# Weight sums staged by whole groups, and four more groups by seven, in a hybrid attention block

## The chip, the cores and the metric

One core of one Trainium2 chip runs the kernel. The metric is the device time in microseconds (us) of the whole kernel, lower is better. Engines are named TensorE (PE in the profile), VectorE (DVE), ScalarE (ACT), GpSimd (POOL) and SyncE (SP, which issues nearly all DMAs).

## The reference

Everything is float32; `S` = 256 tokens, `D` = 2048. Cut to what matters:

```python
h = rms_norm(x, g_mix)
proj = h @ w_in                                   # 2048 x 11014: three attentions' inputs and the gates
o_fox, o_sb, o_mem = forgetting(...), stick_breaking(...), memory(...)   # 6, 6 and 4 heads of 128
g = sigmoid(gates.reshape(b, s, 3, D) + b_gate)
merged = g[0] * (o_fox @ w_br_fox) + g[1] * (o_sb @ w_br_sb) + g[2] * (o_mem @ w_br_mem)
x = x + merged @ w_out                            # 2048 x 2048
u = causal_depthwise_conv(rms_norm(x, g_ffn) @ w_up, conv_w, conv_b)     # 2048 x 11264, 3 taps
u_gate, u_val = split(u, 2)
x = x + (silu(u_gate) * u_val) @ w_down           # 5632 x 2048
```

## The kernel before, in words

**Products.** Each float32 matrix is split in two parts, `hi` (rounded by a cast on ScalarE) and `lo` (the rest, subtracted on VectorE). A product of two matrices is three matmuls, high by high, low by high and high by low (`three`, lines 284 to 288). Weights arrive in pieces of 1024 columns per partition (512 KB): a DMA on SyncE into one of four `raw` slots, a cast into one of four `hi` slots, a subtraction into one of four `lo` slots, then TensorE. The four slots are how far the supply may run ahead.

**Stages, in order.** Memory keys and values with the transposes of `x`; the projections `mq`, `f0` to `f4`, `s0` to `s4` (16 k-tiles each, by twos); the gates and the branch products; the output stage (`w_out`, 16 groups); the up stage (`w_up` with convolution); the down stage (`w_down`, 44 groups). In the last stages a group is a pair of k-tiles against 1024 output columns and both token tiles.

**Groups by eight and by seven.** The plans (`o_plans`, `g_plans`, `d_plans`, lines 225 to 227) give a letter for each step. `e`: a group by the ordinary eight block products (`eight`, line 346). `s`: a group by seven, in Winograd's form of Strassen's scheme (`seven`, line 369): it multiplies sums of weight blocks with sums of activation blocks and collects four of its products in four more banks `Y`, which `gather` (line 305) folds into the residual after the last `s` of a half. A group by seven needs three and a half pieces of weights where one by eight needs two. `f` (`form`, line 1213): VectorE and ScalarE form the activation sums of one group (`pair_sums`, line 290), in `sf` or in place of activations that are no longer needed.

**Weight sums ahead of time.** The sums of weight blocks that `seven` reads are made beforehand and kept in DRAM (`sums_of`, tiles `kept_o`, `kept_d`). `weight_sums` (line 243) is a generator that works on half a group (256 columns of each block) at a time: two loads into a 4 KB per partition tile `pre`, three additions on VectorE, one store.

**Who does it when.** `tick` is called after each piece pair of a product, that is after every second k-tile of a projection or of the up stage. It advances every generator in `background` by one `yield`, and at most two of the queue `later` (heads, transposes, `x_sums`). So `period`, `store`, `add` and `delay` count ticks. `in_order` fixes an instruction's place among those so marked; the others are placed by the scheduler. In gate blocks no background generator is advanced. Before, one generator runs from `mq` to the end of the branches with period 6 (8 from the first gate block on), and two, with a tile each (`end0`, `end1`, which later hold the last activations), run in the up stage with period 8, store at tick 6, and delays of 22 and 24 ticks.

**Slots.** Tiles with one tag share a slot, and the later waits for the earlier one's last use. `xres` first holds `x`, then the activation sums `xs` of the gates, then `x` again. `x_sums` (line 842) forms `xs` after the forgetting heads.

Of the kernel before, what the change touches and what calls it, by code (L numbers as in the profile page):

```python
# [9 lines left out]
F32 = mybir.dt.float32  # L10
# [5 lines left out]
P = 128  # L16
# [19 lines left out]
BLOCKS = 14  # L36
WINDOW = 2
GS = 3


@with_exitstack
def hybrid_block(
# [54 lines left out]
    def later(gen):  # L97
        waiting.append(gen)
# [24 lines left out]
    def finish():  # L123
        while waiting or active:
            tick(beside=False)
# [96 lines left out]

    o_plans = ("eessesse", "eesesese")
    g_plans = (("", "", "esesesee"), ("esesesee", "esesesee", "esesesee"))
    d_plans = ("ef" * 5 + "ssef" * 4 + "seeee", "efefefesssfe" + "ssse" * 2 + "ssssee")
    T1, T3, T4, T2 = range(4)
    FS2, FS4, FS3, FS1 = range(4)
    in_order = tc.keep_in_program_order  # L230
# [9 lines left out]
        for h in range(2)  # L240
    )

    def weight_sums(staging, period, store, end=None, delay=0, slower=0, add=0):


        for _ in range(delay):
            yield
        while halves and end not in issued:
            name, wv, nb, pr, h = halves.popleft()
            at = f"{name}{nb}_{pr}"  # L250
            if h == 0:
                sums_of[name, nb, pr] = dram.tile([P, 4, 512], F32, tag=f"kept_{at}", name=f"kept_{at}")
            kept = sums_of[name, nb, pr]
            w = staging(f"pre_{at}_{h}").rearrange("p (i c) -> p i c", i=4)
            n0 = nb * PIECE + h * 256
            for n in range(2):
                in_order(
                    nc.sync.dma_start(
                        w.rearrange("p (k n) c -> p k n c", k=2)[:, :, n],
                        wv[:, 2 * pr : 2 * pr + 2, n0 + n * 512 : n0 + n * 512 + 256],  # L260
                    )
                )

            for _ in range(add):
                yield
            both = w[:, 1:2].to_broadcast([P, 2, 256])
            in_order(nc.vector.tensor_tensor(w[:, 0:2], w[:, 0:4:3], both, ALU.add))
            in_order(nc.vector.tensor_tensor(w[:, T2], w[:, T1], w[:, T2], ALU.add))
            in_order(nc.vector.tensor_tensor(w[:, T4], w[:, T2], w[:, T4], ALU.add))
# [20 lines left out]
    def pair_sums(pair, w, groups):  # L290

        v = pair.bitcast(F32).rearrange("p k (l c) -> p k l c", l=2)
        a, r = (half.rearrange("p (i q) -> p i q", i=4) for half in (w[:, :512], w[:, 512:]))
        nc.vector.tensor_tensor(w[:, :512].rearrange("p (k c) -> p k c", k=2), v[:, :, 0], v[:, :, 1], ALU.add)

        a10 = a[:, 1:2].to_broadcast([P, 2, P])
        nc.vector.tensor_tensor(r[:, FS3 : FS1 + 1], a[:, 0:4:3], a10, ALU.subtract)
        nc.vector.scalar_tensor_tensor(r[:, FS2], r[:, FS1], -1.0, a[:, 0], ALU.mult, ALU.subtract)
        nc.vector.tensor_tensor(r[:, FS4], r[:, FS2], a[:, 2], ALU.add)
        for dst, which in groups:  # L300
            nc.scalar.copy(dst[..., 0, :], r[:, which])
        for dst, which in groups:
            nc.vector.tensor_tensor(dst[..., 1, :], r[:, which], dst[..., 0, :].bitcast(F32), ALU.subtract)
# [143 lines left out]
    mv = mem[0].rearrange("(t p) d -> p t d", p=P)  # L447
    memres = xt_pool.tile([P, NT, D], F32, tag="xt", name="memres")

    def load_rows(q, srcs, name):  # L450

        n = sum(r for _, r in srcs)
        rows = cst.tile([n, P], F32, name=f"rows_{name}")
# [43 lines left out]
    taps = cst.tile([P, 4, 2 * FT], F32, name="taps")  # L497

    def constants():
        rows = cst.tile([2 * KT + 4, P], F32, name="rows_mix")  # L500
# [220 lines left out]
    def weighted(pT, v, h, oh, o):  # L721
# [6 lines left out]


    ps = proj(C_MQ, MEM_W, "mq")  # L730
    background.append(
        weight_sums(lambda name: gp.tile([P, 1024], F32, tag="pre", bufs=1, name=name), 6, 4, "merged", slower=2, add=2)
    )
    finish()
    qm = heads_of(block("qm"))
    y = norm_heads(ps, rstd, "mq")
    later(heads_T(y, qm, (gh[:, 2:3], gh[:, 2:3]), 2, "mq"))
# [99 lines left out]
        yield  # L837
        weighted(pT, vf, h, h, A)

    xs = cst.tile([P, GS, 4, 2, P], F32R, tag="xres", name="xs")  # L840

    def x_sums():
        for p in range(GS):
            pair_sums(xT.pair(p), block(f"xw_{p}"), [(xs[:, p], slice(0, 4))])
            yield 2

    later(running_sums())
    for h in range(N_FOX):
        later(fox_head(h))
    later(x_sums())  # L850


    qs = [None] * 3
    vs = [None] * 2
# [51 lines left out]
        later(sb_head(h))  # L906

    ps = proj(C_SB + 1536, 512, "s3")
    vs[0] = rows_of(block("vs0"))
    for t in range(NT):  # L910
        nc.scalar.activation(vs[0][:, t], ps[t], AF.Copy, scale=rstd[:, t : t + 1])
# [117 lines left out]


    hT = k_tiles("hT")
    rbc = cst.tile([P, S], F32, name="rbc")

    def hidden_T(n):
        yield
# [42 lines left out]

    FA = FT - 4
    aT = ff.tile([P, FA, 2 * S], F32R, bufs=1, name="aT")  # L1080
    ends = {}
    for i in range(2):
        background.append(
            weight_sums(
                lambda name, i=i: ff.tile([P, 1024], F32, tag=f"end{i}", bufs=1, name=name), 8, 6, delay=22 + 2 * i
            )
        )

    def a_pair(p):
        if p < FA // 2:  # L1090
            return aT[:, 2 * p : 2 * p + 2]
        if p not in ends:
            ends[p] = ff.tile([P, 2, 2 * S], F32R, tag=f"end{p - FA // 2}", bufs=1, name=f"end_{p}")
        return ends[p]

    uv = ctx.enter_context(ExitStack())
    cp = uv.enter_context(tc.tile_pool(name="cp", bufs=2))
# [115 lines left out]
    def form():  # L1213
        p = formed[0]
        formed[0] += 1
        if p < N0:
            groups = [(sf[:, p], slice(0, 3))]
# [56 lines left out]
```

## Time and profile before

| what | value |
|---|---|
| median of 3 runs | 1467.25 us (1466.77 to 1467.32) |
| the profiled execution's own time | 1466.63 us |
| span, first to last instruction | 1464.9 us |
| TensorE, VectorE, ScalarE busy | 1459.6, 1192.2, 839.0 us |
| DMA moved, mean rate | 369.55 MB, 252 GB/s |
| granted TensorE clock | 1.00 |

The span is taken from one profiled execution, and its own time is a little longer, because something lies before the first and after the last instruction. Busy times are unions of instruction durations; TensorE's durations overlap, since matmuls are pipelined, so its share says only that it is never without one. The numbers behind `x` are instruction counts. In a row of waits stand the total, the number of times and the longest wait.

### The profile page before, as it was taken

To read this page: it belongs to the slowest core of one execution; us is meant where nothing else is said; L and a number is where in the kernel's file an instruction comes from. 1 tells how busy PE (TensorE), PEld (TensorE's weight loads), DVE (VectorE), ACT (ScalarE), POOL (GpSimd) and SP (SyncE) were. 2 spreads that over 40 slices of the span, in tenths; PEclk is the share of its full clock that TensorE was granted. 3 is DMA by queue.
4 is the path that set the end of the run, shared out by engine and by line. 5 is a ranking of instruction groups with operands and counts; after the bars stand their busy time and mean duration, and the time that the engine had idled before them with its cause. 6 is when DMAs were issued, how large, how long until landed. Compare 5 with 4: busy or idle time off the path is not lost.

```text
span 1464.9 us, 20666 instructions
## 1 busy us (share of the span) xinstructions
PE 1459.6 (100%) x7335; PEld 1235.3 (84%) x7335; DVE 1192.2 (81%) x1816; ACT 839.0 (57%) x1194; POOL 21.7 (1%) x48
## 2 busy tenths in 40 slices
PE   9999999999999999999999999999999999999998
PEld 7888888888888888888888888888888888888887
DVE  5777676776588899997877889888888887997887
ACT  6755454464364455546666656556556556674664
POOL 0000000021000000000000000000000000000000
PEclk9999999999999999999999999999999999999999
DMA  9686787687868576778777889888888876798796
GB/s 309 198 281 189 222 279 218 186 265 217 258 190 281 169 222 203 270 260 279 257 194 229 276 281 294 276 282 289 288 285 284 277 235 196 254 319 267 263 333 215
DMA packets 205606, 369.55 MB, mean 252 GB/s; under 512 B 13578, under 2 KB 82078, under 8 KB 205246
## 3 DMA queue, kind: packets, MB, share of 16 engines
q1 hardware_dynamic: 204094, 365.99, 78.3%
q10 hardware_dynamic: 1328, 2.11, 0.4%
q8 instruction: 57, 0.93, 0.2%
q14 instruction: 47, 0.39, 0.1%
q0 software_dynamic: 80, 0.13, 0.0%
HBM read 335.67 MB, written 32.51 MB: 251 GB/s over the span
## 4 chain that ended last, share of the span: by engine, by line
PE 99%; DVE 0%; ACT 0%; POOL 0%; issue 0%; POOLq 0%; DVEq 0%
PE u L1174 22%; PE u L1175 11%; PE xd L288 4%; PE xd L287 4%; PE xd L286 4%; PE xg L286 3%; PE xg L287 3%; PE xg L288 3%; PE f L288 2%; PE f L286 2%; PE f L287 2%; PE s L286 2%; PE s L288 2%; PE s L287 2%; PE g L286 2%; PE b L286 2%
## 5 line engine op out<-in xcount | busy, mean ns | idle before, releaser
L1174 PE MATMUL u<-hT,hi_u 128*128 128x512 f32 x1232 | 428.3, 394 | 0.0
L1175 PE MATMUL u<-hT,lo_u 128*128 128x256 f32 x1232 | 341.4, 277 | 0.0
L1174 PEld LDWEIGHTS u<-hT,hi_u 128*128 128x128 f32 x1232 | 231.0, 188 | 53.6
L142 DVE TENSOR_TENSOR lo_u<-raw_u,hi_u 128x1024 fp32r<-128x1024 f32 x176 | 214.9, 1221 | 63.8 <-ACT hi_u L141 62.9
L141 ACT CAST hi_u<-raw_u 128x1024 fp32r<-128x1024 f32 x176 | 184.8, 1051 | 137.1 <-PE u L1174 120.5
L1175 PEld LDWEIGHTS u<-hT,lo_u 128*128 128x128 f32 x1232 | 231.3, 188 | 0.0
L281 DVE TENSOR_TENSOR lo_d<-raw_d,hi_d 128x1024 fp32r<-128x1024 f32 x88 | 106.8, 1223 | 20.2 <-ACT hi_d L280 17.5
L280 ACT CAST hi_d<-raw_d 128x1024 fp32r<-128x1024 f32 x88 | 91.8, 1053 | 47.6 <-PE xd L287 22.2
L280 ACT CAST hi_g<-raw_g 128x1024 fp32r<-128x1024 f32 (+1 forms) x64 | 61.7, 972 | 37.7 <-PE xg L287 12.4
L281 DVE TENSOR_TENSOR lo_g<-raw_g,hi_g 128x1024 fp32r<-128x1024 f32 (+1 forms) x64 | 70.9, 1117 | 4.3 <-ACT hi_g L280 4.3
L141 ACT CAST hi_f<-raw_f 128x1024 fp32r<-128x1024 f32 (+1 forms) x40 | 38.5, 966 | 52.1 <-PE f L287 47.3
L142 DVE TENSOR_TENSOR lo_f<-raw_f,hi_f 128x1024 fp32r<-128x1024 f32 (+1 forms) x40 | 44.7, 1119 | 27.9 <-ACT hi_f L141 25.9
L287 PE MATMUL xd<-hi_d,aT 128*128 128x512 f32 x170 | 66.2, 389 | 0.0
L286 PE MATMUL xd<-hi_d,aT 128*128 128x512 f32 x170 | 66.2, 389 | 0.0
L288 PE MATMUL xd<-lo_d,aT 128*128 128x512 f32 x170 | 66.2, 389 | 0.0
L142 DVE TENSOR_TENSOR lo_s<-raw_s,hi_s 128x1024 fp32r<-128x1024 f32 (+1 forms) x40 | 44.7, 1117 | 25.2 <-ACT hi_s L141 24.6
L141 ACT CAST hi_s<-raw_s 128x1024 fp32r<-128x1024 f32 (+1 forms) x40 | 38.4, 961 | 43.9 <-PE s L287 27.1
L1174 PE MATMUL u<-hT_rest,hi_u 128*128 128x512 f32 x176 | 62.0, 394 | 0.0
L1125 ACT ACTIVATE y<-u,taps 128x256 f32<-128x256 f32 x88 | 49.6, 596 | 17.0 <-DVE u L1120 16.9
L142 DVE TENSOR_TENSOR lo_g<-raw_g,hi_g 128x1024 fp32r<-128x1024 f32 x32 | 39.3, 1232 | 22.9 <-ACT hi_g L141 22.4
L141 ACT CAST hi_b<-raw_b 128x1024 fp32r<-128x1024 f32 x32 | 33.5, 1052 | 40.5 <-PE b L287 13.5
L141 ACT CAST hi_g<-raw_g 128x1024 fp32r<-128x1024 f32 x32 | 33.6, 1050 | 37.7 <-PE g L287 34.8
(482 smaller groups left out, 3533.7 us busy)
## 6 DMA issues: line engine op xcount, KB each, us to landing
raw_u<-in_w_up_dram SPq DMA_DIRECT2D x176, 512.0 KB, 5.1
raw_g<-in_w_in_dram SPq DMA_DIRECT2D x96, 512.0 KB, 4.3
raw_d<-in_w_down_dram SPq DMA_DIRECT2D x66, 512.0 KB, 5.1
pre_d<-in_w_down_dram SPq DMA_DIRECT2D x88, 256.0 KB, 4.5
kept_d<-pre_d SPq DMA_DIRECT2D x44, 512.0 KB, 6.1
raw_f<-in_w_in_dram SPq DMA_DIRECT2D x32, 512.0 KB, 4.7
raw_s<-in_w_in_dram SPq DMA_DIRECT2D x32, 512.0 KB, 3.8
raw_o<-in_w_out_dram SPq DMA_DIRECT2D x25, 512.0 KB, 5.5
```

The source lines that it names most:

```text
L141: pin(nc.scalar.copy(hi[:, :m], raw[:, :m]))
L142: pin(nc.vector.tensor_tensor(lo[:, :m], raw[:, :m], hi[:, :m].bitcast(F32), ALU.subtract))
L280: nc.scalar.copy(hi[:, :n], src)
L281: nc.vector.tensor_tensor(lo[:, :n], src, hi[:, :n].bitcast(F32), ALU.subtract)
L286: fix(nc.tensor.matmul(o, lhsT=ah, rhs=w[0], start=first, stop=False))
L287: fix(nc.tensor.matmul(o, lhsT=al, rhs=w[0], start=False, stop=False))
L288: fix(nc.tensor.matmul(o, lhsT=ah, rhs=w[1], start=False, stop=last))
L1125: nc.scalar.activation(y, u[:, 2:], AF.Identity, scale=tap(2), bias=tap(3))
L1174: nc.tensor.matmul(ps[i], lhsT=hi[:, j, c], rhs=hT(k + j), start=first, stop=False)
L1175: nc.tensor.matmul(ps[i][:, :S], lhsT=lo[:, j, c], rhs=hT(k + j)[:, :S], start=False, stop=last)
```

## The change

Four things change together.

1. The plans: the second half of the output stage gets a fourth group by seven (8 of 16 in all); the down stage gets 11 and 14 instead of 9 and 13 (25 of 44), in another order, with 11 and 3 form steps instead of 9 and 4.
2. `weight_sums` is split. `pair_sums_ahead` works on a whole group: one load of 1 MB, three additions twice as wide, one store. It runs from `f0` to the end of `s3` in two turns of an 8 KB tile `staged` in x's slot (period `PF` = 6, sums at tick 3, store at tick 5), and in the up stage in one tile `ends` that is later the last activations (period 8, sums at tick 1, store at tick 5, delay `DU` = 22). `half_sums`, by halves, runs only beside the first gates and the branches (period 8).
3. `x_sums` moves from the queue of heads to the background of the first gate projections, six ticks after `s4`, with `junk` tiles for its temporaries.
4. The activation sums of the down stage get 28 places in `sf`; the other places of the tenth and eleventh group are in a tile of the down pool and in the slots of `rbc`, `taps` and the constants' rows, which share tags for that.

```diff
+PF = 6
+DU = 22
-    o_plans = ("eessesse", "eesesese")
+    o_plans = ("eessesse", "eessesse")
     g_plans = (("", "", "esesesee"), ("esesesee", "esesesee", "esesesee"))
-    d_plans = ("ef" * 5 + "ssef" * 4 + "seeee", "efefefesssfe" + "ssse" * 2 + "ssssee")
+    d_plans = (
+        "efefefef" + "sef" * 4 + "ssefsfssfssee",
+        "efefef" + "sss" + "esss" * 3 + "ssee",
+    )
...
-    def weight_sums(staging, period, store, end=None, delay=0, slower=0, add=0):
...
+    def sums_in(w):
+        both = w[:, 1:2].to_broadcast([P, 2, w.shape[2]])
+        in_order(nc.vector.tensor_tensor(w[:, 0:2], w[:, 0:4:3], both, ALU.add))
+        in_order(nc.vector.tensor_tensor(w[:, T2], w[:, T1], w[:, T2], ALU.add))
+        in_order(nc.vector.tensor_tensor(w[:, T4], w[:, T2], w[:, T4], ALU.add))
+
+    def half_sums(staging, period, add, store, end):
...
-            for _ in range(period - store + (slower if "heads" in issued else 0)):
+            for _ in range(period - store):
+                yield
+
+    def pair_sums_ahead(staging, period, add, store, end=None, delay=0):
+
+        for _ in range(delay):
+            yield
+        while len(halves) > 1 and halves[0][-1] == 0 and end not in issued:
+            name, wv, nb, pr, _ = halves.popleft()
+            halves.popleft()
+            kept = kept_for(name, nb, pr)
+            w = staging(f"pre_{name}{nb}_{pr}")
+            in_order(
+                nc.sync.dma_start(
+                    w.rearrange("p (k c) -> p k c", k=2), wv[:, 2 * pr : 2 * pr + 2, nb * PIECE : (nb + 1) * PIECE]
+                )
+            )
+            w = w.rearrange("p (i c) -> p i c", i=4)
+            for _ in range(add):
+                yield
+            sums_in(w)
+            for _ in range(store - add):
+                yield
+            in_order(nc.sync.dma_start(kept, w))
+            for _ in range(period - store):
                 yield
...
     ps = proj(C_MQ, MEM_W, "mq")
-    background.append(
-        weight_sums(lambda name: gp.tile([P, 1024], F32, tag="pre", bufs=1, name=name), 6, 4, "merged", slower=2, add=2)
-    )
     finish()
+    staged = cst.tile([P, 2, 2 * PIECE], F32, tag="xres", name="staged")
+    turn = [0]
+
+    def in_turn(name):
+        turn[0] += 1
+        return staged[:, turn[0] % 2]
+
+    background.append(pair_sums_ahead(in_turn, PF, 3, 5, "s3"))
...
-    later(x_sums())
...
     issued.add("vs1")
+    for g in background:
+        deque(g, 0)
+    background.clear()
+    xs = cst.tile([P, GS, 4, 2, P], F32R, tag="xres", name="xs")
+
+    def x_sums():
+        for _ in range(6):
+            yield
+        for p in range(GS):
+            pair_sums(xT.pair(p), (junk(f"xa_{p}"), junk(f"xr_{p}")), [(xs[:, p], slice(0, 4))])
+            for _ in range(3):
+                yield
+
+    background.append(x_sums())
+    background.append(
+        half_sums(lambda name: gp.tile([P, 1024], F32, tag="pre", bufs=1, name=name), 8, 2, 4, "merged")
+    )
...
-    for i in range(2):
-        background.append(
-            weight_sums(
-                lambda name, i=i: ff.tile([P, 1024], F32, tag=f"end{i}", bufs=1, name=name), 8, 6, delay=22 + 2 * i
-            )
-        )
+    ends_tile = lambda name, dt: ff.tile([P, 2, PIECE], dt, tag="ends", bufs=1, name=name)
+    background.append(
+        pair_sums_ahead(lambda name: ends_tile(name, F32).rearrange("p i c -> p (i c)"), 8, 1, 5, delay=DU)
+    )
...
-    sf = xt_pool.tile([P, N0, 3, 2, P], F32R, tag="xt", name="sf")
+    sf = xt_pool.tile([P, 28, 2, P], F32R, tag="xt", name="sf")
...
-        if p < N0:
-            return sf[:, p, f]
+        if p < 9:
+            return sf[:, 3 * p + f]
+        if p == 9:
+            return sf_more[0][:, f] if f < 2 else sf_rest[2]
+        if p == 10:
+            return sf[:, 27] if f == 0 else sf_rest[f - 1]
```

More of the change, by code (lines that the diff above doesn't have):

```diff
@@ L241, in hybrid_block, with kept_for @@
     )
-    def weight_sums(staging, period, store, end=None, delay=0, slower=0, add=0):
-        for _ in range(delay):
-            yield
+    def sums_in(w):
[3 more added lines that the diff above has]
+        in_order(nc.vector.tensor_tensor(w[:, T4], w[:, T2], w[:, T4], ALU.add))
+    def kept_for(name, nb, pr):
+        if (name, nb, pr) not in sums_of:
+            at = f"kept_{name}{nb}_{pr}"
+            sums_of[name, nb, pr] = dram.tile([P, 4, 512], F32, tag=at, name=at)
+        return sums_of[name, nb, pr]
+    def half_sums(staging, period, add, store, end):
         while halves and end not in issued:
             name, wv, nb, pr, h = halves.popleft()
[L250 to L254, printed above, removed]
+            kept = kept_for(name, nb, pr)
+            w = staging(f"pre_{name}{nb}_{pr}_{h}").rearrange("p (i c) -> p i c", i=4)
             n0 = nb * PIECE + h * 256
@@ L448, in hybrid_block @@
     memres = xt_pool.tile([P, NT, D], F32, tag="xt", name="memres")
+    all_rows = cst.tile([2 * KT + 4, 2, P], F32, tag="rows", name="all_rows")
     def load_rows(q, srcs, name):
-        n = sum(r for _, r in srcs)
-        rows = cst.tile([n, P], F32, name=f"rows_{name}")
+        rows = all_rows[: sum(r for _, r in srcs), 0]
         at_row = 0
@@ L496, in hybrid_block @@
     gh = cst.tile([P, 4], F32, name="gh")
[L497 removed]
+    taps = cst.tile([P, 4, 2 * FT], F32, tag="taps", name="taps")
     def constants():
[L500 removed]
+        rows = all_rows[:, 1]
         nc.sync.dma_start(rows[:KT], tiles_of(g_mix[0]))
@@ L838, in fox_head @@
         weighted(pT, vf, h, h, A)
[L840 to L845, printed above, removed]
     later(running_sums())
@@ L1091, in a_pair @@
             return aT[:, 2 * p : 2 * p + 2]
-        if p not in ends:
-            ends[p] = ff.tile([P, 2, 2 * S], F32R, tag=f"end{p - FA // 2}", bufs=1, name=f"end_{p}")
-        return ends[p]
+        if not ends:
+            ends.append(ends_tile("a_ends", F32R).rearrange("p i (k c) -> p i k c", k=2))
+        return ends[0][:, p - FA // 2]
     uv = ctx.enter_context(ExitStack())
@@ L1215, in form @@
         formed[0] += 1
-        if p < N0:
-            groups = [(sf[:, p], slice(0, 3))]
+        if p == 9:
+            sf_rest.extend(cst.tile([P, 2, P], F32R, tag=tag, name=f"sf_{tag}") for tag in ("rbc", "taps", "rows"))
+        if p < 9:
+            groups = [(sf[:, 3 * p : 3 * p + 3], slice(0, 3))]
+        elif p == 9:
+            sf_more.append(place([P, 2, 2, P], F32R, "sf", "sf_more"))
+            groups = [(sf_more[0], slice(0, 2)), (sf_rest[2], 2)]
         else:
```

18 lines of the change are left out of this document (10 added, 8 removed).

## The prediction

> **What bounds the kernel now.** I read the page's busy times and its chain first, then the waits, then the busy time by stage, then single rows of the down stage.
>
> ```profile
> span 1464.9 us, 20666 instructions
> PE 1459.6 (100%) x7335; PEld 1235.3 (84%) x7335; DVE 1192.2 (81%) x1816; ACT 839.0 (57%) x1194; POOL 21.7 (1%) x48
> ...
> PE 99%; DVE 0%; ACT 0%; POOL 0%; issue 0%; POOLq 0%; DVEq 0%
> ```
>
> TensorE is 99% of the chain that ended last. A busy share alone would not prove that it never waits, so the next question is what its suppliers waited for. These are rows of the waits: the first two of the whole span, the third of the down stage alone, the fourth of SyncE's queue.
>
> ```profile
> ACT hi_u L141 <- PE u L1174: 120.5, 106, 1.9
> ACT hi_u L141 <- DMA raw_u<-in_w_up_dram: 7.0, 3, 5.6
> ACT hi_d L280 <- DMA raw_d<-in_w_down_dram: 2.5, 2, 1.7
> SPq L258 <- DMA kept_d<-pre_d: 48.4, 35, 4.7
> ```
>
> ScalarE, which casts the weights, waits for TensorE to free a `hi` slot (106 times) and almost never for data (3 times). The supply runs ahead of TensorE. The stages, in order: forgetting and stick-breaking projections, output stage, up stage, first and second half of the down stage; then four close-ups.
>
> ```profile
> 87.00:300.00 213.00, 213.00 (x1069) 180.49 (x1068) 151.46 (x268) 102.14 (x166) 4.57 (x12) 1.00 0.73 224
> 653.00:746.00 93.00, 93.00 (x424) 77.21 (x423) 77.25 (x95) 55.73 (x70) 0.00 (x0) 1.00 0.77 250
> 746.00:1238.00 492.00, 492.00 (x2843) 430.29 (x2842) 418.60 (x723) 295.14 (x454) 1.43 (x2) 1.00 0.85 266
> 1238.00:1352.00 114.00, 114.00 (x505) 94.43 (x504) 102.87 (x154) 70.49 (x91) 0.00 (x0) 1.00 0.83 276
> ...
> 300.00:310.00 10.00, 9.85 (x76) 9.41 (x74) 7.43 (x12) 8.01 (x14) 2.71 (x4) 1.00 0.88 299
> 1268.00:1306.00 38.00, 38.00 (x170) 31.46 (x169) 37.82 (x57) 27.62 (x37) 0.00 (x0) 1.00 0.91 299
> 1385.00:1445.00 60.00, 60.00 (x267) 49.70 (x266) 46.71 (x43) 40.01 (x43) 0.00 (x0) 1.00 0.97 333
> 1425.00:1435.00 10.00, 10.00 (x46) 8.29 (x45) 6.53 (x7) 5.58 (x7) 0.00 (x0) 1.00 1.02 381
> ```
>
> After the stretch come TensorE, weight loads, VectorE, ScalarE and GpSimd; the last three numbers are the granted clock, the DMA share and GB/s. TensorE is busy for all of each large stage at clock 1.00. So time falls only with TensorE's own work, and rises only where a supplier loses its lead. Two suppliers are near their end: VectorE in the first down half (37.82 of 38 us) and the DMA engines in the runs by seven (share 0.97 and 1.02). In both places TensorE still lost nothing.
>
> **The change, part by part.** First the pitch of a matmul, from TensorE's timeline, with the VectorE operation that makes one of its operands:
>
> ```profile
> 1394.83 0.39 PE L286 MATMUL yd<-hi_t_d,sf 128*128 128x512 f32 x1
> ...
> 1399.36 0.39 PE L288 MATMUL yd<-lo_t_d,aT 128*128 128x512 f32 x1
> ...
> 1399.81 0.39 PE L287 MATMUL yd<-hi_t_d,sf 128*128 128x512 f32 x1
> 1396.57 1.83 DVE L281 TENSOR_TENSOR lo_t_d<-raw_t_d,hi_t_d 128x1024 fp32r<-128x1024 f32 x2
> ```
>
> There are 22 steps from the first matmul shown to the last: (1399.81 − 1394.83)/22 = 0.2264 us each. The 0.39 us durations overlap.
>
> *Four more groups by seven.* A group by eight issues 2 × 2 × 2 × 3 = 24 matmuls of 512 columns, one by seven 7 × 3 = 21. The output stage goes from 7 to 8 groups by seven, the down stage from 22 to 25. That is 4 × 3 = 12 matmuls fewer: 12 × 0.2264 = **−2.72 us**, all on the path, since TensorE sets the time there. The Trainium skill, "TensorE: Matmul & The Clock Gate", section "Back-to-back issue gap", gives about 216 ns for an isolated 512-column matmul and about 131 ns sustained; by these the gain would be 2.59 or 1.57 us. The trace's 226 ns disagrees with both and decides.
>
> *What the suppliers pay for them.* VectorE's groups of the down half 1252 to 1350, and the staging sums of the up stage:
>
> ```profile
> L281 DVE TENSOR_TENSOR lo_d<-raw_d,hi_d 128x1024 fp32r<-128x1024 f32 x39 | 47.2, 1222 | 5.8 <-ACT hi_d L280 5.1
> L294 DVE TENSOR_TENSOR fw<-aT 128x512 f32<-128x512 f32 x10 | 6.9, 689 | 0.1
> L281 DVE TENSOR_TENSOR lo_t_d<-raw_t_d,hi_t_d 128x512 fp32r<-128x512 f32 x9 | 6.2, 690 | 1.7 <-PE yd L287 1.1 <-ACT hi_t_d L280 0.6
> L303 DVE TENSOR_TENSOR sf<-fw,sf 128x384 fp32r<-128x384 f32 x9 | 5.0, 554 | 0.4 <-ACT sf L301 0.4
> L297 DVE TENSOR_TENSOR fw<-fw 128x256 f32<-128x256 f32 x10 | 4.2, 423 | 0.1
> L298 DVE SCALAR_TENSOR_TENSOR fw<-fw 128x128 f32<-128x128 f32 x10 | 2.9, 290 | 0.1
> ...
> L267 DVE TENSOR_TENSOR pre_d<-pre_d 128x512 f32<-128x512 f32 x35 | 23.9, 682 | 0.0
> L268 DVE TENSOR_TENSOR pre_d<-pre_d 128x256 f32<-128x256 f32 x35 | 14.8, 422 | 0.9
> L269 DVE TENSOR_TENSOR pre_d<-pre_d 128x256 f32<-128x256 f32 x35 | 14.8, 422 | 0.9
> ```
>
> By durations a group by eight costs VectorE 2 × 1.222 = 2.44 us, one by seven 3 × 1.222 + 0.690 = 4.36, and a form step (`f`: one 512, one 256, one 384 and three 128 wide) 0.689 + 0.423 + 0.554 + 3 × 0.290 = 2.54. TensorE takes 24 × 0.2264 = 5.43 and 21 × 0.2264 = 4.75 us. In the first down half two groups move from eight to seven and two form steps are added: 2 × 1.92 + 2 × 2.54 = +8.9 us on VectorE. Its 102.87 us become 111.8, in 114 − 2 × 0.68 = 112.6 us. Durations overstate (successive operations overlap by a few hundredths), but VectorE is nearly full. Lost there: at least 0, as in 1268:1306, where VectorE was 99.5% busy and TensorE lost nothing. At most: VectorE idled 0.18 us of 38, or 0.5 us in 112, so 111.8 + 0.5 does fit; but the plan's `sfssfss` needs 5 × 4.36 + 2 × 2.54 = 26.9 against 5 × 4.75 = 23.8, a debt of 3.1 us if no form step runs earlier. The lead that pays it: above, the first of two `lo_t_d` ends near 1397.8 and is read at 1399.36, 1.6 us later. I take **+0.2 us**, near the lower end, which has the row of the same stage; both ends stay for the range. The second half trades one form step (−2.54) for one group (+1.92), and the output stage pays +1.92 on 77.25 of 93: nothing lost.
>
> *Staging while the projections run.* Half a group costs VectorE 0.682 + 2 × 0.422 = 1.53 us, a whole one by the 1024 and 512 wide rows 1.22 + 2 × 0.68 = 2.58. The 72 ticks from `f0` to `s3` take 12 whole groups instead of about 12 halves: +12.6 us, less the three x sums that leave (3 × (0.689 + 0.423 + 2 × 0.290 + 0.68) = 7.1): 151.46 becomes 157 of 213, 74%. DMA: a half moves 1.05 MB in and out, a whole group twice that, so 12 × 1.05 = 12.6 MB more in 213 us: 224 becomes 283 GB/s. VectorE at 85% and 266 GB/s, in the up stage, is the nearest row with TensorE unhurt: cost 0. The cover is the lead of the weights; were it gone, the bill would be TensorE idle for each pair's transfer. New waits: the first pair's load on x's slot (its last ScalarE readers) and the x sums' writes on the last store from it. Behind the load stand `raw_f` loads on SyncE; behind the x sums' writes, casts of gate weights. The x sums move into the first gate projections, done some 20 ticks before the block that reads them.
>
> *Staging in the up stage.* 17 whole groups replace 35 halves: 35 × 1.53 − 17 × 2.58 = 9.7 us less on VectorE, and SyncE issues 34 DMAs instead of 105. But one tile serves where two took turns: each load waits for the previous store to land, three ticks after its issue (before: two ticks, per tile), and the `raw_u` loads stand behind it on SyncE. A tick is 492/176 = 2.8 us. SyncE waited here before, 35 times, 4.7 us at most, and TensorE was busy 492.00 of 492. I take 0.
>
> Sum: −2.72 + 0.2 = **−2.5 us**. The profiled execution took 1466.63 us (span 1464.9 and 1.7 around it) and becomes 1464.1; it stood 0.6 below the median of the three runs, so 1467.25 − 2.5 = **1464.7**. About 0.2%, 2.9 us, is what a measurement of this kernel can tell from no change; the whole credible gain of the arithmetic, 2.72 us, lies just inside it.
>
> **The rivals.** *A: more than the arithmetic, about 1464.0.* Taking the x sums out of the queue of heads lets the stick-breaking heads start earlier and mixes them otherwise with projections. The matmuls there are not all at their pitch:
>
> ```profile
> L286 PE MATMUL s<-hi_s,xT 128*128 128x512 f32 x112 | 46.0, 411 | 0.0
> ...
> L287 PE MATMUL s<-hi_s,xT 128*128 128x512 f32 x112 | 43.7, 390 | 0.0
> ```
>
> The first pass is (411 − 390) × 112 = 2.4 us slower than the second, and at 300:310 TensorE idles 0.15 us at the first head. If 0.7 us of this goes, the gain is 2.72 + 0.5 and passes 0.2%. Against it: nothing in the change removes a transpose.
>
> *B: VectorE starves TensorE in the first down half.* If most of the 3.1 us debt is paid by TensorE, say 2.6, the time is 1467.25 − 2.72 + 2.6 = 1467.1. For it: 111.8 of 112.6 us. Against it: 1268:1306.
>
> *C: the DMA engines bind in the two runs of five by seven.* One such group loads 3.5 × 0.524 = 1.835 MB in 4.75 us, 386 GB/s. At 1385:1445's 333 GB/s for a share of 0.97 the engines carry 343, so a group takes 5.35 us: 10 × 0.6 = 6 us, less what the six raw slots hold. With 2.5 us of that covered: 1467.25 − 2.72 + 3.5 = 1468.0. Against it: 381 GB/s at 1425:1435, TensorE 10.00 of 10. The Trainium skill, "DMA: Bandwidth & Descriptors", section "Specifications", puts HBM at about 358 GB/s for a core; by that ten groups would lose 3.7 us. The 381 lies above it.
>
> *D, the slower side: the one tile of the up stage.*
>
> ```profile
> pre_d<-in_w_down_dram SPq DMA_DIRECT2D x88, 256.0 KB, 4.5
> kept_d<-pre_d SPq DMA_DIRECT2D x44, 512.0 KB, 6.1
> ```
>
> A whole store is twice `kept_d`: at most 2 × 6.1 = 12.2 us to land, against 3 × 2.8 = 8.4 us until the next load's turn. SyncE would then stand 3.8 us, 17 times. TensorE pays only beyond what the lead covered before, 4.7 us. From an excess of 0.33 us each (17 × 0.33 = 5.6 = 2.7 + 2.9) the kernel is slower by over 0.2%. At 1 us each: 1464.5 + 17 = 1481.5. For it: the tile is single and the load behind it is twice as large as well. Against it: 12.2 already takes the fixed part of a DMA twice, and 3.8 is under 4.7.
>
> **How the numbers follow.** Forecast 0.36, A 0.32, B 0.10, C 0.06, D 0.16. A alone is faster by over 0.2%: 0.32. Forecast, B and C lie within: 0.52. D with lesser accidents: 0.16. The forecast's own range is 1464.4 to 1465.3. The whole reaches down to A with the runs' spread (0.55 us between lowest and highest): 1463.6; and up to C: 1468.0. D is left out.
>
> **What would show it.** Right: 12 matmuls fewer on TensorE (x7323); every large stage with TensorE as busy as its length; the first down half 1.3 us shorter with VectorE above 97%; no `raw_u` wait longer than 5.6 us on ScalarE; DMA near 283 GB/s where it was 224. Wrong: TensorE idle around the last five groups by seven of either down half (B or C, told apart by whether `hi_d` waits for a DMA), regular gaps every eight ticks of the up stage (D), or a shorter first 400 us (A).

## The result, and the profile after

The changed kernel takes 1464.87 us (median; 1463.78 to 1466.92), the kernel before 1466.8 us (1466.19 to 1470.32) beside it: a ratio of 0.9987, interval 0.9981 to 0.9992. The forecast was 1464.7 us and −2.5 us; the change brings −1.9 us. The interval lies wholly below 1, so the gain is there, but it is inside the 0.2% (2.9 us) that I called no change. The profiled execution took 1465.37 us.

The page of the changed kernel, with its span, its busy times and the chain that ended last:

```profile
span 1463.3 us, 20524 instructions
PE 1456.8 (100%) x7323; PEld 1231.9 (84%) x7323; DVE 1198.0 (82%) x1768; ACT 845.7 (58%) x1205; POOL 20.3 (1%) x48
...
PE 98%; DMA 1%; DVE 0%; issue 0%; ACT 0%; SPq 0%; DVEq 0%
```

There are 7323 matmuls, 12 fewer, as computed. But the chain has a new member, DMA with 1%, that is 11 us, of which the transfer found below makes 7.3: somewhere TensorE now waits for a transfer. The busy time by stage of the changed kernel finds it (after the stretch TensorE, weight loads, VectorE, ScalarE, GpSimd, granted clock, DMA share, GB/s):

```profile
87.00:300.00 213.00, 212.46 (x1061) 179.29 (x1060) 163.16 (x274) 105.19 (x172) 7.61 (x16) 1.00 0.80 273
653.00:746.00 93.00, 93.00 (x423) 77.20 (x423) 77.14 (x91) 57.32 (x72) 0.00 (x0) 1.00 0.79 254
746.00:1238.00 492.00, 492.00 (x2842) 430.32 (x2842) 410.66 (x672) 293.70 (x453) 1.43 (x2) 1.00 0.82 264
1238.00:1352.00 114.00, 114.00 (x504) 94.38 (x504) 109.40 (x169) 75.26 (x102) 0.00 (x0) 1.00 0.87 288
...
198.00:210.00 12.00, 11.46 (x56) 9.22 (x55) 8.18 (x13) 6.57 (x7) 0.00 (x0) 1.00 0.89 315
```

In the projections TensorE is no longer busy throughout: 212.46 of 213 us, and the whole gap of 0.54 us lies in 198:210, where the short projection `f4` (262 columns) meets `s0`. The chain of the changed kernel around it (start us, us, what):

```profile
188.35 1.23 DVE staged L250
...
191.35 0.70 DVE staged L252
...
192.07 0.34 SPq L303
...
192.50 7.30 DMA raw_s<-in_w_in_dram
...
199.82 1.06 ACT hi_s L143
...
200.90 1.24 DVE lo_s L144
...
202.18 0.50 PE s L319
```

SyncE is about to issue the store of a staged pair (line 303) and must wait for its sums on VectorE, which end at 192.05. The weights of `s0` stand behind the store on SyncE, need 7.30 us to land, then a cast and a subtraction, and TensorE stands.

To keep the accounts by stage free of the first 60 us, whose length differs by about 2 us between executions, I took the time from the first matmul of each stage to that of the next (the last column: to the last matmul), from the traces of all kernels, in us:

| kernel | s0 to gates | gates, branches | output | up | down |
|---|---|---|---|---|---|
| before | 116.65 | 352.11 | 85.04 | 489.95 | 224.66 |
| changed | 117.06 | 352.47 | 84.36 | 489.95 | 222.69 |
| changed, again | 117.27 | 351.98 | 84.36 | 489.95 | 222.69 |
| staging_alone | 117.17 | 352.33 | 85.04 | 489.95 | 224.66 |
| x_sums_moved | 116.23 | 352.54 | 85.04 | 489.95 | 224.69 |
| store_at_6 | 117.58 | 352.42 | 84.36 | 489.95 | 222.68 |
| pause_f4 | 116.23 | 351.98 | 84.36 | 489.95 | 222.69 |
| form_extra | 117.23 | 351.98 | 84.36 | 489.95 | 223.92 |
| up_store_7 | 117.11 | 352.69 | 84.36 | 489.95 | 222.69 |
| up_store_8 | 117.24 | 352.17 | 84.36 | 489.95 | 222.69 |
| paused_26 | 116.24 | 352.01 | 84.36 | 501.41 | 221.99 |
| early_25 | 116.24 | 352.03 | 84.35 | 502.06 | 222.67 |
| late_26 | 116.24 | 352.00 | 84.36 | 512.98 | 221.99 |
| phase_26 | 116.23 | 351.98 | 84.36 | 489.95 | 222.01 |

The projections `f` take 111.26 or 111.27 us in every one. The two lines of the changed kernel show what one program varies by: half a microsecond in the gates and branches, 0.2 in `s0` to the gates. A stage can lose more than its idle time shows: a matmul's duration (0.39 us) is longer than its pitch (0.2264), so a wait of up to 0.16 us leaves TensorE "busy". The 0.54 us of idle time at `f4` go with 0.83 us in the stage.

### The profile page after: what moved, and what is told of

Its sections match the earlier page's. It is cut to its first block, busy times and chain, and to the rows that moved or that the text cites. A ratio compares the mean times of both kernels' runs of the same rounds, so it can differ in the third digit from the quotient of the medians.

```text
span 1463.3 us, 20524 instructions
## 1 busy us (share of the span) xinstructions
PE 1456.8 (100%) x7323; PEld 1231.9 (84%) x7323; DVE 1198.0 (82%) x1768; ACT 845.7 (58%) x1205; POOL 20.3 (1%) x48
## 4 chain that ended last, share of the span: by engine, by line
PE 98%; DMA 1%; DVE 0%; issue 0%; ACT 0%; SPq 0%; DVEq 0%
PE u L1219 22%; PE u L1220 11%; PE xd L318 3%; PE xd L319 3%; PE xd L317 3%; PE xg L319 3%; PE xg L317 3%; PE xg L318 3%; PE f L317 2%; PE f L318 2%; PE f L319 2%; PE s L319 2%; PE s L317 2%; PE s L318 2%; PE g L317 2%; PE b L317 2%
## 5 line engine op out<-in xcount | busy, mean ns | idle before, releaser
L319 PE MATMUL xd<-lo_d,aT 128*128 128x512 f32 x148 | 57.6, 389 | 0.0
L317 PE MATMUL xd<-hi_d,aT 128*128 128x512 f32 x148 | 57.6, 389 | 0.0
L318 PE MATMUL xd<-hi_d,aT 128*128 128x512 f32 x148 | 57.6, 389 | 0.0
```

What stands on the lines that cost most here:

```text
L317: fix(nc.tensor.matmul(o, lhsT=ah, rhs=w[0], start=first, stop=False))
L318: fix(nc.tensor.matmul(o, lhsT=al, rhs=w[0], start=False, stop=False))
L319: fix(nc.tensor.matmul(o, lhsT=ah, rhs=w[1], start=False, stop=last))
```

## The experiments

**The staging alone.** The changed kernel with the plans of before, so that everything but the groups by seven is there.

```
-    o_plans = ("eessesse", "eessesse")
+    o_plans = ("eessesse", "eesesese")
-    d_plans = ("efefefef" + "sef" * 4 + "ssefsfssfssee", "efefef" + "sss" + "esss" * 3 + "ssee")
+    d_plans = ("ef" * 5 + "ssef" * 4 + "seeee", "efefefesssfe" + "ssse" * 2 + "ssssee")
```

> The changed staging, x sums and slots, with the plans of before (7 and 22 groups by seven, 7335 matmuls). Theory T (the gain is the 12 matmuls; the staging itself costs TensorE one wait of 0.7 us where the last projection of the forgetting part, with its short ticks, meets s0, and gives back the 0.5 us that TensorE idled at the first stick-breaking head): no gain, within 0.5 us of the kernel before, TensorE idle about 0.5 us near 202 us. Rival U (the staging by whole groups is what gains, the groups by seven are eaten up by VectorE): faster than before by 1.5 to 2 us.

Measured: 1467.37 us, ratio 1.0004 (0.9995 to 1.0012). The output and down stages are those of before to the hundredth, and the wait where `f4` meets `s0` is there, as in the changed kernel:

```profile
198.00:210.00 12.00, 11.47 (x55) 9.15 (x54) 7.94 (x12) 6.58 (x7) 0.00 (x0) 1.00 0.90 319
```

So the gain is the matmuls', and the staging gives nothing by itself.

**The x sums moved alone.** The kernel before, with its `x_sums` in the background of the first gates.

```
-    later(x_sums())
+    background.append(x_sums())      # six ticks after s4, three ticks apart, behind issued.add("vs1")
```

> The kernel before with one part of the change: the x sums formed in the background of the first gate projections. Theory T: the wait of TensorE at the first stick-breaking head (0.42 us at 308 us) vanishes and nothing else moves: 0.3 to 0.6 us less than before. Rival X (rival A of the prediction in full): the heads mix better with the projections and more than 1 us goes.

Measured: 1466.24 us, ratio 0.9995 (0.9986 to 1.0004), which the time can't tell from none. The trace can. First the kernel before, then this one, in the stretch of the first stick-breaking head:

```profile
300.00:312.00 12.00, 11.85 (x84) 11.07 (x83) 9.43 (x16) 9.74 (x17) 3.39 (x6) 1.00 0.79 255
```

```profile
300.00:312.00 12.00, 12.00 (x93) 11.67 (x93) 7.51 (x12) 7.40 (x11) 1.08 (x4) 1.00 0.81 258
```

The idle 0.15 us is gone, and the stage is 0.42 us shorter (116.23 against 116.65), the same amount as in every later kernel without the `f4` wait. Rival A's mechanism is real, at 0.4 us in that stage. In the same trace the gates and branches took 0.43 us more than in the kernel before, which is within what one program varies by there, so a gain of the whole kernel is not shown by this run alone.

**The staging paused in `f4`.** The generator is taken out of the background while `f4` is issued; the up stage then starts at tick 14 instead of 22, for one pair more.

```
-DU = 22
+DU = 14
+    resting, background[:] = background[:], []
     ps = proj(2048, 262, "f4")
+    background[:] = resting
```

> The changed kernel with its staging paused in the eight short ticks of f4; 11 whole groups instead of 12 are staged before s3's end, 18 instead of 17 in the up stage (delay 14 instead of 22). Theory T: the wait near 202 us is gone, TensorE busy for all of 198 to 210 us, 0.5 to 0.8 us less than the changed kernel, about 1464.1. Rival V (the wait there belongs to the turn from f4 to s0 with its value and logit steps, not to the staging): it stays, same time as the changed kernel.

Measured: 1463.75 us, ratio 0.9976 (0.9967 to 0.9985). The stretch has no gap:

```profile
198.00:210.00 12.00, 12.00 (x59) 10.05 (x58) 6.28 (x11) 5.88 (x9) 0.00 (x0) 1.00 0.86 311
```

0.83 us come back in that stage (117.06 to 116.23), 1.04 against the other execution of the changed kernel. The staging did cost what I had taken as nothing, and only there.

**The store a tick later.** In the projections, store at tick 6 instead of 5, so that the sums are long done when SyncE comes to the store.

```
-    background.append(pair_sums_ahead(in_turn, PF, 3, 5, "s3"))
+    background.append(pair_sums_ahead(in_turn, PF, 3, 6, "s3"))
```

> The changed kernel with the store of each pair, in the projections, at tick 6 instead of 5: the same bytes, but the sums have a tick more before SyncE comes to the store. Theory T (SyncE stands behind the store for VectorE's sums, with the raw_s loads behind it): the wait near 202 us shrinks by the length of a short tick, 1.5 us, that is it vanishes; about 0.5 us less than the changed kernel. Rival W (the DMA engines are full there, whatever the order): the wait stays at 0.5 us or more.

Measured: 1465.51 us, ratio 0.9991 (0.9982 to 1.0). The wait didn't go; it came earlier and grew:

```profile
190.00:202.00 12.00, 10.96 (x66) 9.49 (x65) 8.02 (x11) 5.89 (x10) 0.00 (x0) 1.00 0.99 340
```

With the store at tick 6 of a period of 6, the 1 MB store and the next 1 MB load go out back to back, DMA is at a share of 0.99, and the pieces of weights behind them land late: the first of `s0` in 6.8 us, where the changed kernel has 3.95. So "SyncE stands behind the store" was too narrow a cause. What the two kernels have in common is the supply in `f4`: a piece is twelve matmuls, at 0.122 us each for 262 columns (the pitch in these traces) where a full one has 0.2264, so it keeps TensorE for 1.46 us instead of 2.7, and a lead of a number of pieces shrinks while `f4` runs. The traces show it. SyncE issues the last piece of `f3` 18.3 us before its first matmul and the first piece of `s0` 8.75 us before, in the kernel before; in the changed kernel and in `store_at_6` it is 18.6 and 8.75. (18.6 us are almost seven full pieces: the slots of `raw` and those of `hi` and `lo` add up, so the supply runs further ahead than four.) The piece that comes late in the changed kernel, the fourth of `s0`, is issued 8.5 us before its first matmul (12.35 in the kernel before) and needs 7.30 us to land, 1.06 for the cast and 1.24 for the subtraction. In `pause_f4` SyncE stands 3.7 us for the sums of a pair too, but at 197 us, where the pieces are long again, and TensorE loses nothing. An `f4` with pieces of full length was not tried, and `pause_f4` also moves the staging that follows, so the short pieces are the reading on which these three kernels agree, not a cause taken out by itself.

**The up stage's store at tick 7 and at tick 8** (instead of 5, period 8): the next load then asks for the tile one tick after the store, or at once.

```
-        pair_sums_ahead(..., 8, 1, 5, delay=DU)
+        pair_sums_ahead(..., 8, 1, 7, delay=DU)      # up_store_7; 8 in up_store_8
```

> The changed kernel with each store of the up stage one tick instead of three ahead of the next load into the same tile. Theory T (rival D is wrong because SyncE's wait stays below the lead of the weights): SyncE waits for the store's landing each time, some 6.1 - 2.8 = 3.3 us or a little more instead of 1.8, and TensorE stays busy for all of the up stage: same time within 0.5 us. Rival D: the lead is spent, and each of 17 pairs costs TensorE 0.5 us or more, 8 us in all.

> The changed kernel with each store of the up stage right ahead of the next load into the same tile (no tick between). Theory T as the prediction had it: SyncE waits for the whole landing, about 6.1 us or more, 1.4 us beyond the 4.7 us that cost nothing before, so TensorE loses about 17 x 1.4 = 24 us. Rival Y: the lead is longer than 4.7 us (four raw and four hi slots of 2.8 us each), and nothing or under 3 us is lost.

Measured: 1465.67 and 1465.16 us, one execution each, without an interval. The waits of SyncE's queue in the up stage for `up_store_8` (total, times, longest), and TensorE there:

```profile
SPq L293 <- DMA kept_d<-pre_d: 65.6, 16, 5.4
```

```profile
746.00:1238.00 492.00, 492.00 (x2843) 430.18 (x2842) 411.12 (x672) 294.16 (x453) 1.43 (x2) 1.00 0.81 264
```

SyncE now stands 65.6 us in all, 4.1 each, 5.4 at most, with `raw_u` loads behind it, and the stage lasts 489.95 us as always. My theory's 24 us fell; the rival, that the lead covers it, holds.

**One more operation in each form step.** A second 512 wide addition for VectorE, about 0.7 us, in each of the 14 form steps; it computes the same values again.

```
+        nc.vector.tensor_tensor(fw[:, :512]..., v[:, :, 0], v[:, :, 1], ALU.add)
         pair_sums(a_pair(p), fw, groups + [(s_of(p, FS1), FS1)])
```

> The changed kernel with one more VectorE operation in each form step of the down stage (the 512-wide sum is made twice): 11 x 0.6 = 7 us more of VectorE in the first down half, 2 us in the second. Theory T (VectorE is nearly full there: 109.4 of 114 us busy): it now has more to do than the half lasts, and TensorE loses 2 to 5 us, all of it in the first down half. Rival Z (VectorE's share overstates, form steps slip into gaps and can be late): under 0.5 us lost.

Measured: 1466.38 us, ratio 0.9995 (0.9985 to 1.0004); the down stage takes 223.92 us instead of 222.69. Rows of `form_extra` for the first half and for the place where TensorE waits, then of the changed kernel at that place:

```profile
1238.00:1352.00 114.00, 113.89 (x500) 93.17 (x499) 111.42 (x176) 74.83 (x101) 0.00 (x0) 1.00 0.86 283
...
1320.00:1380.00 60.00, 59.89 (x262) 48.12 (x261) 58.89 (x93) 39.67 (x57) 0.00 (x0) 1.00 0.91 302
```

```profile
1320.00:1380.00 60.00, 60.00 (x267) 49.64 (x266) 55.06 (x75) 39.05 (x51) 0.00 (x0) 1.00 0.90 305
```

11 such operations in the first half are some 7.6 us (at the 0.689 us of the prediction's row), and TensorE pays 1.23 over the whole stage, 0.9 of it in the first half. In the changed kernel VectorE has about 5 us of room in these 60; with the extra work it has one, and TensorE begins to pay. The direction was right, the size expected was too large.

**A 26th group by seven.** On top of `pause_f4`; the second half's plan has one group by seven more and one form step more. The extra pair of weight sums is made by an earlier start of the up stage's staging.

```
-DU = 14
+DU = 6
-        "efefef" + "sss" + "esss" * 3 + "ssee",
+        "efsss" * 4 + "esssee",
```

> The version with the staging paused in f4, with one more group by seven: 15 instead of 14 in the second down half (26 of 44), its runs by seven cut to threes between single groups by eight, four form steps instead of three there; 19 groups staged in the up stage (delay 6). Theory T (time falls by the matmuls left out while no supplier loses its lead): three matmuls fewer, 0.7 us less than the paused version, TensorE busy throughout the second down half. Rival: VectorE with a form step more and the DMA engines give it back, or the earlier start of the staging stalls the first up blocks: the same or more.

Measured: 1468.01 us (1464.61 to 1476.09), ratio 1.0021 (1.0003 to 1.0038), a miss. The down stage did gain its 0.7 us (221.99), but the up stage grew to 501.41 us. Either the early start or the extra group could have done that; three more kernels tell them apart.

**The early start alone**: `pause_f4` with `DU = 6` and its 25 groups.

> pause_f4 with its 25 groups by seven, but the up stage's staging begins at tick 6 instead of tick 14, as in paused_26. Theory (the early start alone did paused_26's harm): TensorE waits for weights between 780 and 830 us, then a pair of matmuls of the up stage takes about 353 ns instead of 347, and the time is 3 to 10 us above pause_f4's 1463.75, with a wide spread. Rival (the 26th group did it): the up stage stays near 490 us and the time is within 0.5 us of pause_f4's.

Measured: 1475.17 us (1466.4 to 1477.8), ratio 1.0048 (1.003 to 1.0067). It was the start. `early_25`, where the waits are and far behind them, then the changed kernel there:

```profile
790.00:818.00 28.00, 25.48 (x142) 21.43 (x141) 27.23 (x49) 18.53 (x30) 0.00 (x0) 1.00 0.81 278
...
1010.00:1110.00 100.00, 100.00 (x568) 86.68 (x567) 82.70 (x131) 56.45 (x84) 0.00 (x0) 1.00 0.84 275
```

```profile
790.00:818.00 28.00, 28.00 (x163) 24.47 (x163) 28.00 (x50) 19.93 (x34) 0.00 (x0) 1.00 0.83 272
...
1010.00:1110.00 100.00, 100.00 (x578) 87.46 (x578) 85.42 (x143) 59.55 (x93) 0.00 (x0) 1.00 0.85 287
```

Two things are to be seen. In 790:818 VectorE is about full in both kernels (it catches up on the convolutions), and in `early_25` TensorE stands 2.52 us there. Why, the stretch before shows; first a wait of SyncE's queue in `early_25`, then the same stretch of the changed kernel:

```profile
SPq L293 <- DMA kept_d<-pre_d: 10.2, 1, 10.2
```

```profile
767.00:771.00 4.00, 4.00 (x25) 3.48 (x25) 2.45 (x4) 2.12 (x4) 0.00 (x0) 1.00 1.12 73
771.00:775.00 4.00, 4.00 (x25) 3.52 (x24) 1.99 (x4) 1.32 (x2) 0.40 (x1) 1.00 0.56 40
775.00:779.00 4.00, 4.00 (x25) 3.48 (x24) 0.00 (x0) 0.69 (x1) 0.17 (x1) 1.00 0.80 277
```

Even in the changed kernel the transfers come almost to rest from 767 to 775, at 73 and 40 GB/s, and VectorE finds nothing to do after it. The early store is issued in `early_25` at 767.12, just there; the next load can't go out before 782.22, so SyncE stands 10.2 us, twice what `up_store_8` bore, and the 1 MB load then goes out ahead of the weights that are already late. A start at tick 14 or later keeps the first store out of this hole. That the start does the harm is shown by `early_25` against `pause_f4`; that it does it through this hole is read from the times.

And 200 us later, with TensorE busy 100.00 of 100 us in both at clock 1.00, it issues 568 matmuls where the other issues 578. That is the larger part of the 12 us.

**The 26th group with a later, denser staging**: start at tick 20, period 7.

```
-        pair_sums_ahead(..., 8, 1, 5, delay=DU)      # DU = 14
+        pair_sums_ahead(..., 7, 1, 5, delay=DU)      # DU = 20, and paused_26's plan
```

> pause_f4 with a 26th group by seven (second half of the down stage, 15 instead of 14 groups by seven, four form steps) and with the up stage's staging from tick 20 every 7 ticks instead of from tick 14 every 8, so that the extra group's weight sums are made without the early start of paused_26. Theory (the early start stopped TensorE in paused_26 and left it in a slower rhythm): no wait in the first 100 us of the up stage, that stage near 490 us, three matmuls fewer, 3 x 0.2264 = 0.7 us below pause_f4, about 1463.0 us. Rival (the 26th group or a denser staging in the up stage is itself too much for the suppliers): the up stage is again several us longer, or TensorE waits in the second half of the down stage, and the time is above 1464.5 us.

Measured: 1483.7 us, ratio 1.0112 (1.0097 to 1.0126): far above the 1463.0 of the theory, with an up stage 23 us longer where the rival had several, and my worst miss. Windows of `late_26`, and the wait of SyncE's queue that is new:

```profile
830.00:870.00 40.00, 36.77 (x203) 31.75 (x202) 29.19 (x52) 21.21 (x36) 0.00 (x0) 0.96 0.72 261
...
852.30:855.50 3.20, 3.20 (x12) 2.71 (x11) 2.47 (x3) 0.59 (x1) 0.00 (x0) 0.50 0.92 289
```

```profile
SPq L303 <- DVE aT L178: 18.4, 3, 7.4
```

A block of the up stage is 8 ticks and ends with four convolutions on VectorE. With a period of 8 the sums fall at the same place in each block; with 7 they move through it, and at some places the store waits up to 7.4 us for VectorE, with `raw_u` loads behind it. TensorE then stands 3.2, 3.4 and 3.6 us (from 847, 893 and 1036 us), and with each goes a spell of 3.4 us in which its clock is 0.50. Whether it is the moving place or the 14% denser staging was not separated; VectorE's mean load, 84.63 of 100 us in 910:1010 against 85.41 in the changed kernel, gives no sign of density, but TensorE did less there too (568 matmuls against 579).

**The 26th group in step**: `pause_f4` with start at tick 14 and period 8 kept, and only the plan of the second half changed, as in `paused_26`; the last pair starts two ticks before the end of the staging.

> pause_f4 with the 26th group by seven alone: the up stage's staging keeps its start at tick 14 and its period of 8 ticks, which is also the length of one block of the up stage (8 ticks, then four convolutions), and simply makes one pair more at the end. Theory (the period of 8 keeps the sums at one place between the convolutions, and the start at tick 14 keeps them out of the first blocks; the losses of paused_26, early_25 and late_26 came from the start and from the period of 7): no TensorE wait in the up stage up to its last ten ticks, that stage 490 us, three matmuls fewer than pause_f4: 0.7 us below its 1463.75, about 1463.1 us. Rival (one more pair or one more group is more than the suppliers carry): TensorE waits in the last ten ticks of the up stage, or in the second half of the down stage, and the time is at or above pause_f4's.

Measured: 1463.03 us (1462.57 to 1464.33), ratio 0.9974 (0.9964 to 0.9985); expected were 1463.1. It is the lowest of all the kernels, and clearly below the kernel before; against the changed kernel I compare by their ratios to the same kernel before, 0.9974 against 0.9987. From `pause_f4` (0.9976) the times can't tell it; the stages can. Windows of `phase_26`, the up stage and the two halves of the down stage:

```profile
746.00:1238.00 492.00, 492.00 (x2843) 430.15 (x2842) 415.36 (x678) 293.76 (x453) 1.44 (x2) 1.00 0.81 272
...
1238.00:1352.00 114.00, 114.00 (x505) 94.36 (x504) 109.46 (x169) 75.11 (x102) 0.00 (x0) 1.00 0.88 289
1352.00:1458.00 106.00, 106.00 (x474) 87.94 (x473) 92.25 (x114) 70.35 (x87) 0.00 (x0) 1.00 0.85 298
```

19 staged pairs in the up stage (57 additions, against 51 of the changed kernel's 17) and 15 groups by seven in the second half cost TensorE nothing, and three matmuls fewer are 0.68 us (222.01 against 222.69).

**The changed kernel again**, for the spread.

> The changed kernel once more, beside the other two, for what differs between two executions of one program. Theory: the first matmul of mq moves by up to 1 us, TensorE's wait near 201 us, where the short steps of f4 meet s0, is there again (0.7 us and a small one), the waits in the second gates differ, and the time is within 0.5 us of 1464.9. Rival (the wait at 201 us is an accident of one execution): it is gone or elsewhere.

Measured: 1465.02 us, ratio 0.9988 (0.9979 to 0.9996). The wait is at the same place, TensorE busy 11.47 of 12 us in 198:210; the waits in the second gates, 0.4 us in the first trace, are not there.

## Why the prediction was right, point by point

**TensorE sets the time, a matmul at 0.2264 us: right.** The output stage lost 0.68 us for its three matmuls, the down stage 1.97 of the 2.04 for its nine, `phase_26` 0.68 more for three.

**+0.2 for VectorE in the first down half: about right, nearly nothing.** The last 0.07 of the 2.04 is all that is missing, and the first half is 1.33 us shorter, as its two groups make it (1.36). VectorE came to 109.40 of 114 us, less than my 111.8 in 112.6: 96%, where my sign asked for more than 97%. `form_extra` shows that the edge is near: 7.6 us more in that half, and TensorE pays 1.2 over the stage. My range for the forecast, 1464.4 to 1465.3, was not worked out: the debt of 3.1 us less the lead of 1.6 would have put its upper end at 1466.0. Rivals B and C fall: no TensorE wait lies in the down stage of the changed kernel. Where the last five groups by seven of either half run, the DMA engines are nearly full and TensorE is still busy throughout:

```profile
1300.00:1340.00 40.00, 40.00 (x178) 33.12 (x177) 37.63 (x51) 30.87 (x40) 0.00 (x0) 1.00 0.94 325
1385.00:1445.00 60.00, 60.00 (x266) 49.68 (x265) 47.69 (x44) 42.27 (x47) 0.00 (x0) 1.00 0.96 337
```

**0 for the staging in the projections: wrong by 0.8 to 1.0 us.** My means were fair (VectorE 163 instead of 157 of 213 us, 273 instead of 283 GB/s). The step that failed is "the cover is the lead of the weights": I took all 72 ticks as equal, while those of `f4` are little more than half as long, and the lead falls from 18.6 to 8.75 us while they run. The nearest row, the up stage as a whole, has no short pieces, so it was no bound for this place. `pause_f4` shows the price by taking the staging out of `f4`.

**Rival A: right in its mechanism, hidden in the sum.** The head's wait went and the stage lost 0.42 us, shown by `x_sums_moved` alone. In the changed kernel it pays for half of the `f4` wait. So −2.65 for the matmuls, −0.42 for the heads and +0.83 or +1.04 for `f4` make −2.2 or −2.0. The gates and branches, which vary by themselves, add +0.36 in the first trace of the changed kernel and −0.13 in the second, which makes −1.9 and −2.2 from `s0` on; the medians differ by 1.9. My −2.5 missed by 0.6: two terms that I had at nothing, of opposite sign. That they partly cancel is luck; neither was in my sum.

**0 for the one tile of the up stage: right, though the margin was mis-sized.** Of the changed kernel, issues with their median landing, and the wait of SyncE's queue in the up stage:

```profile
pre_d<-in_w_down_dram SPq DMA_DIRECT2D x17, 1024.0 KB, 7.4
kept_d<-pre_d SPq DMA_DIRECT2D x17, 1024.0 KB, 6.1
```

```profile
SPq L293 <- DMA kept_d<-pre_d: 27.5, 15, 2.7
```

A store of 1 MB lands in 6.1 us, as one of half that size did before; my bound of 12.2 was far too high. The 4.7 us that I set against it was misread: the row that I took it from is of the whole span, and its longest wait lies between 300 and 478 us. In the up stage the kernel before has

```profile
SPq L258 <- DMA kept_d<-pre_d: 36.1, 30, 2.4
```

so the waits became half as many and a little longer (1.8 us each instead of 1.2). Rival D's threshold had no row behind it, and was too low as well: in `up_store_8` 16 waits of 4.1 us each, 5.4 at most, cost nothing. Only one of 10.2, right after the hole in the transfers and ahead of a stretch where VectorE is full, came with a loss. My sign "no `raw_u` wait above 5.6 us" was of no use: the longest was 5.7 us, and TensorE lost nothing.

## What to carry to other kernels

A lead of a fixed number of pieces is as long as the pieces that are in it: cost background work at the shortest piece it runs beside, not at a stage's mean. Keep background work in step with the loop that it runs in, and change its start or period only with the trace beside it; a start eight ticks earlier cost 11 us here, and an extra pair and group kept in step (`phase_26`) gained 0.7 in its trace. When a median moves as forecast, still account by stage: here two terms that I had put at nothing half cancelled.

## What the runs showed of the hardware

**A small transfer, and large ones that land late beside it.** The hole in the transfers above is where two small ones run. Issues of the changed kernel in 760 to 792 us, KB each and median us to landing:

```profile
raw_u<-in_w_up_dram SPq DMA_DIRECT2D x11, 512.0 KB, 4.6
rbc<-rstd_row POOLq DMA_DIRECT2D x1, 128.0 KB, 6.9
rstd_row<-scales POOLq DMA_DIRECT2D x1, 1.0 KB, 9.6
```

1 KB of row scales goes to DRAM, spread over partitions, issued at 764.66 and landing 9.6 us later; while it is under way the engines' share of busy time is 1.12 at 73 GB/s from 767 to 771, and a weight piece issued at 770.40 needs 12.2 us, where the median of these eleven is 4.6. That this transfer is the cause is read from the times alone; it wasn't taken out.

**Two steady rhythms of one stream.** In the up stage 512 and 256 wide matmuls alternate. A pair takes 346.7 ns in the kernel before, the changed kernel and all those with a stage of 489.95 us; after the waits in `paused_26` and `early_25` it takes 353 to 354 ns to the end of the stage, at a granted clock of 1.00 and with no wait in between. In `late_26` it comes and goes: 347 ns after the first wait (860 to 868 us), 353 behind the next ones (from 876), 347 again from 1020, 353 behind the last wait (from 1044), and 347 from 1188 to the end. It ends, without a wait, at 1016 and 1181 us, where three or more 512 wide matmuls stand in a row instead of alternating; such a row at 1061 and at 1087 us did not end it. The 578 and 568 matmuls in 100 us above are the same thing: 1.7%, some 7 us over the rest of the stage. It also shows in the first 5 us of the stage in the kernel before (353 ns), and ends there when transposes come in between. What sets it was not found; the widely spread times of `paused_26` and `early_25` would fit a rhythm that only some executions fall into, which was not tried.

**The clock after a wait.** Three waits of `late_26`, of 3.2, 3.4 and 3.6 us, each came with 3.4 us at a granted clock of 0.50 (852.3 to 855.7, 896.7 to 900.1 and 1040.0 to 1043.5), in which the next matmul followed a 512 wide one after 427 ns. The first spell began 1.6 us after work had begun again, the other two as it began or just before. Its fourth wait, of 1.3 us, and the shorter ones of the other kernels had none. The Trainium skill, "TensorE: Matmul & The Clock Gate", section "What's actually happening", states a half rate after an idle window of about 3.4 us, until about 3.4 us of work; the traces agree, with 3.4 us at 0.50 after waits of 3.2 to 3.6 us. So of `late_26`'s 23 us in the up stage, 11.5 come from standing (its four waits together) and, by estimate from these figures, some 5 from the half clock (three times half of 3.4) and some 5 from the slower rhythm (1.9% of about 270 us).
